# A two-layer trunk on one core: the second norm's sums from x, x·d and d², and residual, norm and split pair by pair into a feature-outermost product

## The chip, the core and the metric

The kernel runs on one core of a Trainium2 chip. The metric is the device time of one execution in microseconds (us). Of the kernel before there are three runs: 2750.5, 2752.84 and 2771.38 us, so a median of 2752.84 us. A change of under about 1% of that, some 27 us, is hardly told from no change by such runs.

## What is computed

Two layers of a transformer-like trunk act on 256 tokens (128 context tokens and 128 latent tokens, the two "groups") with 2048 features. Each layer has two sub-layers, and each of them is wrapped in two RMS norms ("sandwich"):

```python
def rmsnorm(x, g):
    y = x32 * lax.rsqrt(jnp.mean(x32 * x32, axis=-1, keepdims=True) + EPS)
    return y * g

def trunk_layer(x, mod, p, ctx, rope):
    sh1, sc1, g1, sh2, sc2, g2 = jnp.split(mod, 6, axis=-1)
    h = rmsnorm(x, p['g_pre_mix']) * (1.0 + sc1) + sh1
    mix, side = mixers(h, p, ctx, rope)        # in-projection, attention, DFT, recurrent heads
    x = x + g1 * rmsnorm(mix @ p['w_out'], p['g_post_mix'])
    h = rmsnorm(x, p['g_pre_ffn']) * (1.0 + sc2) + sh2
    x = x + g2 * rmsnorm(conv_ffn(h, p), p['g_post_ffn'])
    return x, side
```

The modulation (shift, scale, gate; one set per group) is a product of a conditioning vector with a weight of 2048 x 12288 per layer. Between two sub-layers stand, one behind the other, the norm of the sub-layer's output d, the residual addition, the norm of the new x and the modulation; the next product needs all of it.

## The kernel before

**Layout.** Features lie on partitions and tokens on columns. x is eight tiles `x[k]` of [128, 2, 256] (128x512 elements each; tile k holds features 256k to 256k+255), d is eight tiles `ds[k]` of the same form. A norm over features is thus a sum over partitions, which TensorE does with a matrix of ones.

**Products.** Each fp32 weight is split into two fp32r parts, hi (cast on ScalarE, L343) and lo (subtraction on VectorE, L344), and so is the activation h (`hx`, hi and lo). A product is three terms: hi·hi, hi·lo and lo·hi. `gemm` and `gemm_k` issue three matmuls of 256 columns (L353, L354, L355). `gemm_wide` issues two, one of 512 columns (L382) and one of 256 (L383). `gemm_k` is feature-outermost: it holds several PSUM banks open, takes the features in four pieces of 512 (two tiles of x each) from a generator, and needs a piece only when it comes to it. `gemm_wide` goes through all features for one group of 512 output columns.

**Sums.** `sumsq4` squares a tile on ScalarE (L476) and adds it with two matmuls by ones (L480), each into one of four 32-row strips of a PSUM bank: the matrix of ones has 32 columns there, where the products use 128. `strips` copies the bank (L485) and adds the strips up with one full matmul (L487). `rstd` makes the reciprocal root with two ScalarE operations (L494, L495) and three dependent VectorE operations (L496 to L498).

**Order of the work.** A tile scheduler fixes the order of each engine's instructions when the program is built, and each engine runs its list strictly in order. The modulation's weights are streamed as side work between the products (`mb` L243, `mc` L250, `mod` L255, `modx` L289). `need` takes care that those of a piece are issued by the time that piece is modulated.

**The seams.** There are three places between sub-layers: A (layer 0, mixer to FFN, about 579 to 604 us), B (layer 0 to layer 1, 1469 to 1492 us), C (layer 1, mixer to FFN, 1958 to 1983 us). Ahead of each, the last product adds up the d tiles (L1190 in A and C, L1233 and L1234 in B), and for each tile `done` squares it, sums the square and scales d by the gate (`scale_out`, L552). At the seam `post_norm` makes r1 from these sums, multiplies all d tiles (L545) and adds all into x (L546). Tiles 5 and 6 are done by GpSimd (`POOLX`), the others by VectorE. Then `pre_norm` squares and sums all eight x tiles, makes r2, and yields four pieces. For each tile a piece has four VectorE operations x·scale·r2 of 128x128 (L534), four ScalarE operations that add the shift and cast to hi (L535), and four VectorE operations for lo (L536). `pre_norm` makes the pieces of layer 0's in-projection too, where a piece also waits for its modulation weights. After A and C the first group of the FFN's up-projection is a `gemm_wide`; after B the in-projection is a `gemm_k`, and x is stored to DRAM (`spill_x`, on SyncE's queue). In the mixer x is not on chip; `fill_x` brings it back ahead of the last part of the out-projection.

## Time and profile before

The profile shows one execution of 2751.85 us by its own clock; its span in the trace is 2749.9 us.

| what | value |
|---|---|
| runs | 2750.5, 2752.84, 2771.38 us |
| the profiled execution's own time | 2751.85 us |
| its span | 2749.9 us |
| TensorE (PE) busy | 2648.2 us, 96% |
| weight loads (PEld) busy | 2138.7 us, 78% |
| VectorE (DVE) busy | 1774.9 us, 65% |
| ScalarE (ACT) busy | 1280.8 us, 47% |
| GpSimd (POOL) busy | 123.8 us, 5% |

To read it: the busy time of an engine says little about what a stage is bound by. The stages are read with windows (busy time of each engine between two moments, with TensorE's granted clock: 1.00 is 2.4 GHz, 0.50 is 1.2 GHz) and with the timeline, which lists an engine's instructions in order of time. A row of the timeline that ends with x4 stands for four like records. A plain matmul by ones has two records.

### The profile page before, as it was taken

The numbers are of one execution on the slowest core, as the hardware profiler recorded it, in microseconds if no ns is written. First come the engines' busy times: TensorE is split into PE (matmuls) and PEld (weight loads), VectorE is DVE, ScalarE is ACT, GpSimd is POOL, SyncE is SP. The second block draws the span as 40 slices with busy tenths as digits, with TensorE's granted clock in tenths as the row PEclk, the third lists the DMA queues.
The fourth block names the chain that finished last, engine by engine and source line by source line (L and its number), as shares of the span: only waits on it lengthen the run. The fifth ranks groups of instructions, "written<-read, shape, count | busy, mean of one in ns | idle before, by whom it ended". The sixth has DMA issues, their size and how long they took to land. (4 is left out here: it accounts for less than half of the span.)

```text
span 2749.9 us, 46006 instructions
## 1 busy us (share of the span) xinstructions
PE 2648.2 (96%) x18307; PEld 2138.7 (78%) x18307; DVE 1774.9 (65%) x3008; ACT 1280.8 (47%) x1985; POOL 123.8 (5%) x130
## 2 busy tenths in 40 slices
PE   7999999989999999999998999999799999999997
PEld 4577778757777777777776987878588888888886
DVE  3477858576564466555667687775777646765675
ACT  2255434245453454434544456343465545554553
POOL 1111000010000000000000020000100000000000
PEclk9999999999999999999998999998899999999998
DMA  9965636768888878888876654443355555655552
GB/s 364 382 200 171 224 119 198 252 233 279 273 266 269 283 268 271 265 275 273 267 258 204 213 186 158 153 134 116 114 183 186 193 190 190 191 190 189 189 186 82
DMA packets 316472, 593.95 MB, mean 216 GB/s; under 512 B 22758, under 2 KB 38146, under 8 KB 316256
## 3 DMA queue, kind: packets, MB, share of 16 engines
q1 hardware_dynamic: 314624, 589.54, 64.7%
q8 instruction: 144, 2.36, 0.3%
q0 software_dynamic: 1632, 1.46, 0.2%
q14 instruction: 72, 0.59, 0.1%
HBM read 583.78 MB, written 7.14 MB: 215 GB/s over the span
## 5 line engine op out<-in xcount | busy, mean ns | idle before, releaser
L344 DVE TENSOR_TENSOR lo<-raw,hi 128x1024 fp32r<-128x1024 f32 (+1 forms) x712 | 855.2, 1202 | 656.1 <-ACT hi L343 620.2
L343 ACT CAST hi<-raw 128x1024 fp32r<-128x1024 f32 (+1 forms) x712 | 734.5, 1032 | 949.5 <-PE wm L382 631.9
L382 PE MATMUL wm<-hx,hi 128*128 128x512 f32 x2816 | 994.6, 397 | 8.4 <-DVE hx L536 7.7
L383 PE MATMUL wm<-hx,lo 128*128 128x256 f32 x2816 | 787.4, 280 | 0.0
L382 PEld LDWEIGHTS wm<-hx,hi 128*128 128x128 f32 x2816 | 528.9, 188 | 174.2 <-issue 37.7
L383 PEld LDWEIGHTS wm<-hx,lo 128*128 128x128 f32 x2816 | 533.0, 189 | 3.2 <-issue 2.5
L382 PE MATMUL wm<-g,hi 128*128 128x512 f32 x1408 | 498.9, 398 | 0.0
L383 PE MATMUL wm<-g,lo 128*128 128x256 f32 x1408 | 395.6, 281 | 0.0
L382 PEld LDWEIGHTS wm<-g,hi 128*128 128x128 f32 x1408 | 264.0, 188 | 83.8 <-issue 24.7
L383 PEld LDWEIGHTS wm<-g,lo 128*128 128x128 f32 x1408 | 266.1, 189 | 7.2 <-issue 7.1
L243 PE MATMUL mb<-raw,cst 128*32 128x512 f32 x1536 | 255.9, 614 | 10.7 <-DVE mod L255 6.3
L353 PE MATMUL mm<-hx,hi 128*128 128x256 f32 x544 | 157.9, 294 | 4.2 <-ACT hx L535 4.2
L355 PE MATMUL mm<-hx,lo 128*128 128x256 f32 x544 | 155.6, 288 | 0.9 <-DVE lo L344 0.9
L354 PE MATMUL mm<-hx,hi 128*128 128x256 f32 x544 | 155.9, 288 | 0.5
L353 PE MATMUL mm<-mx,hi 128*128 128x256 f32 x512 | 155.1, 304 | 0.0
L355 PE MATMUL mm<-mx,lo 128*128 128x256 f32 x512 | 148.0, 291 | 1.3 <-DVE lo L344 1.3
L354 PE MATMUL mm<-mx,hi 128*128 128x256 f32 x512 | 148.6, 291 | 0.0
L353 PEld LDWEIGHTS mm<-hx,hi 128*128 128x128 f32 x544 | 104.4, 194 | 24.9 <-issue 14.0
L353 PEld LDWEIGHTS mm<-mx,hi 128*128 128x128 f32 x512 | 100.4, 196 | 24.9 <-issue 20.3
L355 PEld LDWEIGHTS mm<-hx,lo 128*128 128x128 f32 x544 | 105.0, 193 | 5.7 <-issue 3.5
L354 PEld LDWEIGHTS mm<-hx,hi 128*128 128x128 f32 x544 | 105.3, 194 | 4.8 <-issue 3.4
L559 ACT ACTIVATE u<-us,vec 128x256 f32<-128x256 f32 x176 | 100.4, 596 | 15.0 <-DVE us L1215 11.0
(343 smaller groups left out, 3261.4 us busy)
## 6 DMA issues: line engine op xcount, KB each, us to landing
raw<-in_w_mod SPq DMA_DIRECT2D x384, 512.0 KB, 5.2
raw<-in_ffn_w_up SPq DMA_DIRECT2D x352, 512.0 KB, 4.5
raw<-in_ffn_w_down SPq DMA_DIRECT2D x176, 512.0 KB, 4.3
raw<-in_w_in SPq DMA_DIRECT2D x80, 512.0 KB, 4.9
raw<-in_w_out SPq DMA_DIRECT2D x64, 512.0 KB, 5.1
raw<-in_w_uq SPq DMA_DIRECT2D x16, 384.0 KB, 4.5
raw<-in_w_in SPq DMA_DIRECT2D x16, 320.0 KB, 3.5
raw<-in_w_in SPq DMA_DIRECT2D x16, 256.0 KB, 3.4
```

The lines of the kernel that those rows point to most:

```text
L243: nc.tensor.matmul(b[32 * q:32 * q + 32, :], self.cst[:, 4 * kg + q, :], r[:, f, :], start=kg == 0, stop=kg == 3)
L343: nc.scalar.copy(hi[:, :, 0:w], r)
L344: nc.vector.tensor_tensor(lo[:, :, 0:w], r, hi[:, :, 0:w], op=ALU.subtract)
L353: mm(out, whi, xhi, start=start, stop=False)
L354: mm(out, whi, xlo, start=False, stop=False)
L355: mm(out, wlo, xhi, start=False, stop=stop)
L382: mm(ps[m], hi[:, kk, s], x[:, :, kk, :], start=ki == 0 and k2 == 0 and kk == 0, stop=False)
L383: mm(ps[m][:, 0, :], lo[:, kk, s], x[:, 0, kk, :], start=False, stop=ki == n - 1 and k2 == 1 and kk == 1)
L559: nc.scalar.activation(u[:, m, :], ps[:, m, :], AF.Identity, scale=w1, **kw)
```

## The change

1. Ahead of a seam, `done` now makes three sums for each tile: of d² (unscaled), of scaled d times x, and of scaled d squared. They are two squares on ScalarE (L1223, L1226) and one product on VectorE (L1225), three buffers instead of one, and six matmuls by ones in three strips (`sums3`, L474) instead of two matmuls. The last norm of layer 1 keeps `sumsq4`.
2. At a seam, `between` takes the place of `post_norm` and `pre_norm`. One copy (L480) and three matmuls (`spread3`, L484) give the three totals. r1 comes from the first. Four VectorE operations of 128x256 (L561 to L564) update the kept sum of x², `sx`, by 2·r1·(x·d) + r1²·d², and r2 comes from `sx`. No tile of x is squared or summed. d·r1 (L568) and x+d (L569) are done for the two tiles of a piece, just ahead of its modulation, all on VectorE; GpSimd has no part in it.
3. `modulate` makes h = x·r2 with one VectorE operation of 128x512 (L544), four ScalarE operations of 128x128 in place with two per-partition pointers, scale and shift (L549), one ScalarE cast to hi (L550), and one VectorE subtraction to lo (L551), 128x512 each. This form also stands at the start of layer 0, where `sx` is copied too (L528).
4. The first group of the FFN's up-projection is a `gemm_k` that takes the pieces as they come (`evu0` convolves its result from PSUM directly).

```diff
+    def sums3(self, ps, k, srcs):
+        for j in range(2):
+            for i, t in enumerate(srcs):
+                self.nc.tensor.matmul(ps[32 * i:32 * i + 32, :], self.c(C_ONE, 32), t[:, j, :], start=k == 0 and j == 0, stop=k == 7 and j == 1)
+
+    def spread3(self, ps):
+        nc = self.nc
+        sb = self.half([128, 256], nm="sb")
+        nc.scalar.copy(sb[0:96], ps[0:96])
+        out = [self.bank([128, 256]) for _ in range(3)]
+        for i, o in enumerate(out):
+            r = slice(32 * i, 32 * i + 32)
+            nc.tensor.matmul(o, self.c(C_QS, 128)[r], sb[r], start=True, stop=True)
+        return out
...
+    def modulate(self, l, which, k, rs, before=None):
...
+        for e in range(2):
+            if before:
+                before(2 * k + e)
+            hi, lo = out[e][:, 0], out[e][:, 1]
+            h = self.half([128, 2, 256], nm="h")
+            nc.vector.tensor_tensor(h, self.x[2 * k + e], self.bc(rs, 2), op=ALU.mult)
+            for j in range(2):
+                c = 4 * k + 2 * e + j
+                for g in range(2):
+                    s = slice(128 * g, 128 * g + 128)
+                    nc.scalar.activation(h[:, j, s], h[:, j, s], AF.Identity, bias=self.mod[l][:, sh0 + c, g:g + 1], scale=a[:, c, g:g + 1])
+            nc.scalar.copy(hi, h)
+            nc.vector.tensor_tensor(lo, h, hi, op=ALU.subtract)
+        return out
+
+    def between(self, ds, ss, l, which):
+        tt = self.nc.vector.tensor_tensor
+        tot, xd, dd = self.spread3(ss)
+        r1 = self.rstd(tot, D)
+        t = self.half([128, 256], nm="t")
+        tt(t, dd, r1, op=ALU.mult)
+        self.nc.vector.scalar_tensor_tensor(t, xd, 2.0, t, op0=ALU.mult, op1=ALU.add)
+        tt(t, t, r1, op=ALU.mult)
+        tt(self.sx, self.sx, t, op=ALU.add)
+        r2 = self.rstd(self.sx, D)
+
+        def add(k):
+            tt(ds[k], ds[k], self.bc(r1, 2), op=ALU.mult)
+            tt(self.x[k], self.x[k], ds[k], op=ALU.add)
         for k in range(4):
-            self.need(l, sh0 // 4 + k, sh0 // 4 + 4 + k)
-            out = [self.duo("hx") for _ in range(2)]
...
-                        nc.vector.scalar_tensor_tensor(h[:, j, s], self.x[2 * k + e][:, j, s], a[:, c, g:g + 1], rs[:, s], op0=ALU.mult, op1=ALU.mult)
-                        nc.scalar.activation(hi[:, j, s], h[:, j, s], AF.Identity, bias=sh)
-                        nc.vector.scalar_tensor_tensor(lo[:, j, s], h[:, j, s], sh, hi[:, j, s], op0=ALU.add, op1=ALU.subtract)
-            yield out
+            yield self.modulate(l, which, k, r2, add)
...
         def done(which, k):
...
-            self.sumsq4(pss[0], ds[k], 2 * k)
...
+            sq = [self.half([128, 2, 256], nm="sq") for _ in range(3)]
+            nc.scalar.activation(sq[0], ds[k], AF.Square)
             self.scale_out(l, which, k, ds[k])
+            nc.vector.tensor_tensor(sq[1], ds[k], self.x[k], op=ALU.mult)
+            nc.scalar.activation(sq[2], ds[k], AF.Square)
+            self.sums3(pss[0], k, sq)
...
-                self.finish(self.gemm_wide(i["ffn_w_up"][l], [(512 * gg, 512), (DFF + 512 * gg, 512)], h, range(4), evu))
+                cols = [(512 * gg, 512), (DFF + 512 * gg, 512)]
+                if gg == 0:
+                    self.finish(self.gemm_k(i["ffn_w_up"][l], cols, first, evu0, None))
+                else:
+                    self.finish(self.gemm_wide(i["ffn_w_up"][l], cols, h, range(4), evu))
```

**Where the sums stand.** TensorE's list ahead of seam C (`mm` are the out-projection's products, `ss` the bank of sums, `sq` the squares and products of one tile). In the kernel before, the two matmuls of a tile stand together:

```order
L355 MATMUL mm_19355<-mx_17954,lo_19360 128x256
L353 MATMUL mm_19355<-mx_17954,hi_19359 128x256
L480 MATMUL ss_19243<-sq_19332,const 32x256 x2
L354 MATMUL mm_19355<-mx_17954,hi_19359 128x256
L355 MATMUL mm_19355<-mx_17954,lo_19360 128x256
```

In the changed kernel the six of a tile stand in two places: the first, of the unscaled square, alone among the products, and the other five later, here with the first one of the next tile behind them:

```order
L340 MATMUL mm_19441<-mx_17982,hi_19445 128x256
L474 MATMUL ss_19297<-sq_19402,const 32x256
L341 MATMUL mm_19441<-mx_17982,hi_19445 128x256
...
L1133 MATMUL b_19467<-const,fs_16370 64x128 x2
L474 MATMUL ss_19297<-sq_19403,const 32x256
L474 MATMUL ss_19297<-sq_19404,const 32x256
L474 MATMUL ss_19297<-sq_19402,const 32x256
L474 MATMUL ss_19297<-sq_19403,const 32x256
L474 MATMUL ss_19297<-sq_19404,const 32x256
L474 MATMUL ss_19297<-sq_19428,const 32x256
L340 MATMUL mm_19442<-mx_17982,hi_19445 128x256
```

So a tile's sums interrupt the products more often than before, and only tiles 6 and 7, which end at the seam itself, have theirs in one piece.

**What stands at the seam.** VectorE's list at seam C, from r2 on. In the kernel before all additions are over, and the modulation's operations follow r2 directly (`nt` and `rs` are rstd's, `hx` is what the product reads):

```order
L498 SCALAR_TENSOR_TENSOR rs_19588<-nt_19589,rs_19588 128x256
L534 SCALAR_TENSOR_TENSOR h_19597<-x_19166,modx_103,rs_19588 128x128 x3
L536 SCALAR_TENSOR_TENSOR hx_19595<-h_19597,mod_101,hx_19595 128x128
L534 SCALAR_TENSOR_TENSOR h_19597<-x_19166,modx_103,rs_19588 128x128
L536 SCALAR_TENSOR_TENSOR hx_19595<-h_19597,mod_101,hx_19595 128x128 x3
```

In the changed kernel the additions of the first four tiles stand between the operations that lead to r2, and the subtraction to lo (L551) behind four multiplications by r2 and two by r1:

```order
L564 TENSOR_TENSOR sx_291<-sx_291,t_19661 128x256
L569 TENSOR_TENSOR x_19221<-x_19221,d_17025 128x512
L568 TENSOR_TENSOR d_17276<-d_17276,rs_19654 128x512
L501 SCALAR_TENSOR_TENSOR nt_19667<-rs_19666 128x256
L569 TENSOR_TENSOR x_19222<-x_19222,d_17276 128x512
L502 TENSOR_TENSOR nt_19667<-nt_19667 128x256
L568 TENSOR_TENSOR d_17276<-d_17276,rs_19654 128x512
L503 SCALAR_TENSOR_TENSOR rs_19666<-nt_19667,rs_19666 128x256
L569 TENSOR_TENSOR x_19223<-x_19223,d_17276 128x512
L544 TENSOR_TENSOR h_19677<-x_19220,rs_19666 128x512
...
L568 TENSOR_TENSOR d_17571<-d_17571,rs_19654 128x512 x2
L551 TENSOR_TENSOR hx_19673<-h_19677,hx_19673 128x2x256
```

Ahead of these rows, the four operations that make `sx` (L561 to L564) have three such additions between them.

**A piece at the start of layer 0.** ScalarE's list for layer 0's second piece, in the changed kernel: four operations on the first tile, one on the second, and only then the first tile's cast to `hx`, which TensorE waits for.

```order
L549 ACTIVATE h_671<-h_671,mod_100,modx_102 128x128 x4
L549 ACTIVATE h_679<-h_679,mod_100,modx_102 128x128
L550 CAST hx_669<-h_671 128x2x256
L549 ACTIVATE h_679<-h_679,mod_100,modx_102 128x128 x3
L330 CAST hi_765<-raw_763 128x1024
```

Before, the operation that adds the shift wrote `hx` itself, a quarter of a tile at a time. On VectorE the changed list has the multiplication of the second tile between `mod` and `modx`, on which ScalarE waits:

```order
L544 TENSOR_TENSOR h_671<-x_114,rs_284 128x512
L242 TENSOR_TENSOR mod_100<-mc_653,vec_98 128x8
L544 TENSOR_TENSOR h_679<-x_115,rs_284 128x512
L276 SCALAR_TENSOR_TENSOR modx_102<-mod_100,vec_98 128x8
L551 TENSOR_TENSOR hx_669<-h_671,hx_669 128x2x256
```

What depended on no modulation weight, the multiplication of the first tile, has moved ahead of `mod`.

## Rows read from the trace of the kernel before

**Rows 1.** The page, part 1: busy time and share of each engine.

```profile
PE 2648.2 (96%) x18307; PEld 2138.7 (78%) x18307; DVE 1774.9 (65%) x3008; ACT 1280.8 (47%) x1985; POOL 123.8 (5%) x130
```

**Rows 2.** Windows: PE, PEld, DVE, ACT, POOL busy, granted clock, DMA share, GB/s.

```profile
40.00:155.00 115.00, 110.59 (x742) 70.32 (x740) 43.73 (x84) 29.84 (x48) 7.43 (x15) 0.99 0.94 339
579.00:604.00 25.00, 14.33 (x75) 4.22 (x75) 21.18 (x38) 9.21 (x20) 6.72 (x4) 0.73 0.58 189
604.00:632.00 28.00, 26.87 (x158) 19.71 (x157) 23.84 (x67) 16.37 (x37) 0.00 (x0) 1.00 0.64 215
1469.00:1492.00 23.00, 12.44 (x69) 3.88 (x68) 19.03 (x32) 9.09 (x19) 6.63 (x4) 0.72 0.59 195
1958.00:1983.00 25.00, 10.37 (x47) 3.33 (x48) 19.56 (x34) 9.46 (x21) 6.71 (x4) 0.62 0.11 37
1983.00:2003.00 20.00, 18.38 (x90) 15.31 (x90) 17.56 (x50) 12.23 (x28) 0.00 (x0) 0.88 0.33 106
```

**Rows 3.** Timeline, PE, ahead of seam C: start, us, engine, line, operation [idle before].

```profile
1942.25 0.28 PE L355 MATMUL mm<-mx,lo 128*128 128x256 f32 x1
1942.37 0.28 PE L353 MATMUL mm<-mx,hi 128*128 128x256 f32 x1
1942.58 0.62 PE L480 MATMUL ss<-sq,const 128*32 128x256 f32 x4
...
1943.36 0.28 PE L355 MATMUL mm<-mx,lo 128*128 128x256 f32 x1
```

**Rows 4.** Timeline at seam C, all engines.

```profile
1956.11 1.42 DVE L1190 TENSOR_TENSOR d<-d,mm 128x512 f32<-128x512 f32 x2
...
1957.72 1.15 ACT L476 ACTIVATE sq<-d 128x512 f32<-128x512 f32 x2
1957.85 1.22 DVE L344 TENSOR_TENSOR lo<-raw,hi 128x1024 fp32r<-128x1024 f32 x1 [0.31 <-ACT hi L343]
...
1958.99 1.28 DVE L552 TENSOR_TENSOR d<-d,modx 128x512 f32<-128x512 f32 x2
1959.59 0.37 ACT L485 COPY sb<-ss 128x256 f32<-128x256 f32 x1 [0.73 <-PE ss L480]
...
1961.85 0.47 ACT L494 ACTIVATE rs<-b,eps 128x256 f32<-128x256 f32 x1 [1.89 <-PE b L487]
...
1963.35 0.42 DVE L498 SCALAR_TENSOR_TENSOR rs<-nt,rs 128x256 f32<-128x256 f32 x1
1963.81 2.36 DVE L545 TENSOR_TENSOR d<-d,rs 128x512 f32<-128x512 f32 x2
...
1977.65 0.70 PE L487 MATMUL b<-sb,const 128*128 128x256 f32 x2 [0.47 <-ACT sb L485]
...
1982.18 0.79 PE L382 MATMUL wm<-hx,hi 128*128 128x512 f32 x1 [3.82 <-DVE hx L536]
```

**Rows 5.** Timeline at seams A and B: the last addition into d, the first product.

```profile
578.38 0.68 DVE L1190 TENSOR_TENSOR d<-d,mm 128x512 f32<-128x512 f32 x1
...
603.53 0.51 PE L382 MATMUL wm<-hx,hi 128*128 128x512 f32 x1 [2.08 <-DVE hx L536]
...
1469.11 0.41 DVE L1234 TENSOR_TENSOR d<-d,wm 128x256 f32<-128x256 f32 x1
...
1491.37 1.01 PE L353 MATMUL mm<-hx,hi 128*128 128x256 f32 x3 [3.20 <-ACT hx L535]
```

**Rows 6.** Timeline at the start of layer 0, its second piece.

```profile
77.44 0.17 DVE L255 TENSOR_TENSOR mod<-mc,vec 128x8 f32<-128x8 f32 x1 [0.37 <-PE mc L250]
...
77.67 1.05 PE L243 MATMUL mb<-raw,cst 128*32 128x512 f32 x4 [0.29 <-DVE mod L255]
...
78.23 1.49 ACT L535 ACTIVATE hx<-h,mod 128x128 fp32r<-128x128 f32 x4 [6.62 <-DVE h L534]
...
79.60 0.50 PE L354 MATMUL mm<-hx,hi 128*128 128x256 f32 x1
```

**Rows 7.** Groups by line and form: ACT with two pointer operands, and with one.

```profile
L559 ACT ACTIVATE u<-us,vec 128x256 f32<-128x256 f32 x176 | 100.4, 596 | 15.0 <-DVE us L1215 11.0
L559 ACT ACTIVATE k<-mm,vec 128x256 f32<-128x256 f32 x8 | 3.7, 471 | 2.0 <-DVE k L563 1.3 <-PE mm L355 0.7
```

60 lines of the change are left out of this document (34 added, 26 removed).

## The prediction

> **What bounds the kernel now.** I read the page first: TensorE is busy for 96% of the span [rows 1], so nearly everything is bound by it, and other engines count only where it is idle. Then the windows [rows 2]: the idle time lies in the three seams (PE 14.33 of 25 us in A, 12.44 of 23 in B, 10.37 of 25 in C), a little behind A and C (1.1 us of 28, 1.6 of 20), and at the start, where PE has 110.59 of 115 us and the DMA share is 0.94, so there both are near their limit. The timeline then gives each seam's length, from the end of the last addition into d to the first product [rows 4, 5]: C 1982.18 − 1957.53 = 24.65 us, A 603.53 − 579.06 = 24.47, B 1491.37 − 1469.52 = 21.85. Behind C the granted clock is 0.88 in the mean [rows 2]: the first products run at the lower level, 1.2 GHz. Behind A it is 1.00, since modulation matmuls ran shortly before.
>
> So two questions decide: how much shorter the seams get, and what the longer sums cost where TensorE is busy anyway.
>
> **1. The sums ahead of the seams: +20.1.** Products follow each other every 0.12 us [rows 3]. Around one tile's sums a product that was due 0.24 us after 1942.37 starts 0.99 us after it: the block costs 0.75 us, though its four records take only 0.62. The rest is the passage into the strips and back. Two strips run at once. A second round in the same strips is not in the trace; the nearest row is the four-record block with 512 columns [rows 6], 1.05 us against 0.62 with 256, so another 256 columns in each strip cost 0.43. After the change a tile has a lone matmul (0.75: one matmul or two at once, the passage is the same) and a block of two rounds (0.75 + 0.43 = 1.18) against 0.75 before: +1.18 per tile. In A six tiles are split: +7.1. In B there are seven lone pieces and six blocks for six old blocks: 7 × 0.75 + 6 × 1.18 − 6 × 0.75 = +7.8. In C, where some lone matmuls stand behind the block of the tile before, three lone and six blocks, against four old blocks and one of two tiles, taken as 1.18: 2.3 + 7.1 − 4.2 = +5.2. Together +20.1. (Tiles 6 and 7 of each seam are in part 2.) Lowest: if a lone matmul among products cost nothing, only 18 second rounds remain, +7.7. Highest: the wait in the second rival.
>
> What speaks for the high side of this is a rule of the Trainium skill ("TensorEngine Tiling (Array Packing)", Key Properties): a change of the tiling mode, not of the tile, drains TensorE. By that rule the price goes with the number of interruptions, and the 0.13 us between 0.75 and 0.62 [rows 3] agrees that each has one; without it the sum would be nearer to +8 than to +20.
>
> The extra square and product per tile cost nothing of their own there: about 0.6 us each on engines that are not full.
>
> **2. The seams: −10.4.** I follow C from the last addition, 1957.53 [rows 4]. VectorE has one weight split, then scale, product, scale, product for tiles 6 and 7: 1.54 us until the split ends as now, then four operations of 0.60 to 0.68 (the pair takes 1.28): +4.1. With ScalarE's square beside it and two rounds of sums: +5.5. The copy starts at +5.6. From copy to root it took 2.26 us here (1959.59 to 1961.85), where a table is transposed in between, and would take 0.37 for the copy, 0.70 for the matmul and 0.1 without that: I take 1.9 at C, so +7.5, and 1.2 at A and B. Then from root to r1 1.96 as now (1961.85 to 1963.81): +9.4. Then come four operations of 256 columns at 0.46 and the three additions between them at 0.60: 3.64, so +13.1. For r2 there are three more of 0.46, five additions at 0.60 and the first multiplication 0.68: +18.1. ScalarE does four affine operations. A quarter now takes 1.49/4 with one pointer [rows 6]; a second pointer costs 596 − 471 = 125 ns [rows 7], so four take 1.49 to 2.0, I take 1.75; then the second tile's first (0.4) and the cast (0.6): hi at about +21.0. First product +21.1, against 24.65. The 1.6 us of stalls behind C go too: per piece TensorE has 96 products, 11.5 us, and VectorE about 10 (eight operations of 0.6, four weight splits of 1.22), ScalarE less. C: 21.1 − 24.65 − 1.6 = −5.1.
>
> B is one operation and the rest of a split (1.0) shorter and has the earlier root: 21.1 − 1.0 − 0.7 = +19.4, so −2.5. A is as C with the earlier root, +20.4, and loses 1.1 us of stalls; but its modulation matmuls now run ahead of the long wait, not just before the products, so it will start at 1.2 GHz as C does. Behind C 0.12 of the clock is missing over 20 us: 2.4 us, which I charge to A. A: 20.4 − 24.47 − 1.1 + 2.4 = −2.8. The three make −10.4.
>
> Bounds: if the additions slip in for free where VectorE waits for ScalarE, some 2.5 us per seam less, −18; if each dependent operation takes 0.68 rather than 0.60 and the four affine ones 2.0, 2.5 more each, −3. GpSimd's part in the additions falls away; nothing is queued behind it. At B the eight stores of x to DRAM wait in SyncE's queue for additions that now come up to 12 us after the first product; weights queued behind them are of the second piece, which starts 168 products, 20 us, after the first, and need some 5 us to land. That cover gone, it would cost up to those 5 us. The first FFN group as `gemm_k` streams the same 768 columns per block: nothing.
>
> **3. The start of layer 0: +5.** Four pieces each wait for their modulation weights. Before, the first product that needs lo came 2.16 us after `mod` started (77.44 to 79.60) [rows 6]. After: `mod` 0.17, the second tile's multiplication 0.60, `modx` 0.2, affine operations 1.75 + 0.4, cast 0.6, subtraction 0.68 and handovers 0.3 make 4.7: +2.6 at a piece with nothing else to do. In the first two, modulation matmuls that stand there cover about half (+1.5, +1.1). That is +7.8 for four. The first three lie where the DMA is near its limit [rows 2], so a late product is partly made good; I take half for them: 2.6 + 2.6 = +5. Bounds +2.6 (only the last counts) and +14 (twice the sum, with the clock falling in each gap).
>
> **Sum.** 20.1 − 10.4 + 5 = +14.7 on the profiled execution's own 2751.85 (its span is 2 us shorter) gives 2766.6; the median of the three runs is 1 us above it, so **2767 us**, 0.5% more than before.
>
> **The rivals.**
>
> *The sums are nearly free and the seams give all* (0.22). Strips would let a lone matmul slip between products. Sums +7.7, seams −18, start +2.6: −7.7, 2745 us. For it: only 0.13 of the 0.75 us is passage, and strips do run side by side. Against it: the products wait through the whole block [rows 3]. A share of 0.07 is kept for seams that shrink by 10 us each, below 2725.
>
> *TensorE waits in line for the late product* (0.15). The six matmuls of a tile need scaled d times x, which is last on VectorE, and TensorE runs its list in order. If a weight split of 1.22 us [rows 4] stands ahead of that product each time, 18 tiles wait up to 1.22: +22, so 2789 us, slower by 1.3%. It decides from a mean wait of 0.75 us per tile, which takes 2767 to 2780.4. For it: the list puts the five matmuls only some ten products (1.2 us) behind the lone one. Against it: the scheduler set the list so that the operands should be there.
>
> *The seams do not shrink* (0.13). Eight of the sixteen additions still stand between r1 and the first product, r2 still has its own root, and ScalarE now has five operations where the quarter tiles went one by one. If that eats all: 20.1 + 0 + 5, 2778 us. For it: 8 × 0.60 = 4.8 us remain in the chain. Against it: eight squares with sums, GpSimd's slow operations (one of two of VectorE's takes 2.36 − 0.60 = 1.76 beside it [rows 4]) and half of the additions are gone.
>
> **How the numbers follow.** My forecast has 0.50 and reaches from 2757 to 2779. The first rival goes from 2742 upward for most of its 0.22, the second and third up to 2789. The range 2742 to 2789 leaves out the 0.07 below 2725, some 0.06 between, and about 0.06 above: 8 in 10 inside. About 1% can be told from no change, 2725 to 2780. Faster: the 0.07. Slower: nearly all of the second rival, a third of the third, and a rest of my own, 0.20. Within 1%: 0.73.
>
> **What would show it.** Right in step 1: in the windows ahead of the seams each tile's sums hold the products up twice, about 0.75 and 1.2 us; wrong if products follow a lone sum without a gap, or if the five begin after an idle time that the product L1225 ends. Right in step 2: first products 21, 20.5 and 19.5 us after the last addition at C, A and B, a clock near 0.5 behind A, no idle time in the first FFN group. Right in step 3: PE idle 2.6 us more ahead of layer 0's last piece. The prediction is wrong as a whole if the stage ahead of a seam is not longer, or a seam not shorter.

## The result, and the profile after

The changed kernel takes 2787.12 us in the median of six runs (2784.94 to 2799.71), beside 2765.72 for the kernel before in the same rounds (2750.5 to 2771.38): a ratio of 1.0086, interval 1.0065 to 1.0107. On another chip the same pair gave 1.0127 (1.0103 to 1.015). So the change makes the kernel slower, by 21 us and 30 us between these medians; predicted were 14.7 us, too little to be told from no change. 2787 us lies near the upper end of the wide range (2742 to 2789) and outside the forecast's own 2757 to 2779.

One thing must be known to read any of these numbers: the runs of the kernel before fall into two groups, about 2751 and 2765 us, and the execution profiled ahead of the prediction is of the lower one. A second profile of the same kernel took 2764.83 us. The two differ in layer 1's feed-forward. These are windows over the same 500 us of it; the columns are those of [rows 2]. First the execution of [rows 1]:

```profile
2100.00:2600.00 500.00, 500.00 (x2886) 441.18 (x2885) 320.51 (x426) 257.79 (x334) 0.00 (x0) 1.00 0.59 190
```

The second profile of the kernel before:

```profile
2100.00:2600.00 500.00, 500.00 (x2833) 433.60 (x2832) 314.22 (x419) 252.47 (x330) 0.00 (x0) 1.00 0.62 186
```

The changed kernel:

```profile
2100.00:2600.00 500.00, 500.00 (x2832) 433.56 (x2831) 312.93 (x414) 251.03 (x327) 0.00 (x0) 1.00 0.59 187
```

TensorE is never idle and its granted clock is 1.00 in all three, but 2886 matmuls are done in the first and 2833 and 2832 in the others: a pair of one 512-column and one 256-column product takes 0.347 or 0.353 us. Over the whole of that feed-forward this is 12.6 us. It does not need the change, since both kinds occur in the kernel before. Whether the change makes the faster pace rarer was not tested: 43 of the 113 runs of the kernel before lie below 2758 us, while all sixteen profiles of other builds have the slower pace, and so has one of the changed kernel at 2786.17 us, close to the lowest of its twelve runs. All delays below are therefore taken against the second profile, whose pace is that of the changed kernel's profile (own time 2791.3 us): 2791.3 − 2764.83 = 26.5 us to explain.

Part 1 of the page, of the second profile of the kernel before and then of the changed kernel, answers to [rows 1]. At the same pace TensorE is busy 19 us longer, at the same share (31 us longer than in [rows 1], where the pace is the faster one):

```profile
PE 2660.2 (96%) x18307; PEld 2140.7 (77%) x18307; DVE 1775.8 (64%) x3008; ACT 1280.4 (46%) x1985; POOL 123.7 (4%) x130
PE 2679.2 (96%) x18665; PEld 2163.6 (78%) x18665; DVE 1756.4 (63%) x2849; ACT 1300.5 (47%) x1998; POOL 95.4 (3%) x118
```

Its windows answer to [rows 2]: the start, and for each seam the wait and what follows it.

```profile
40.00:155.00 115.00, 105.67 (x675) 70.63 (x669) 34.34 (x45) 32.81 (x52) 7.43 (x15) 0.93 0.93 332
603.00:623.00 20.00, 9.71 (x62) 3.05 (x62) 17.20 (x36) 7.09 (x17) 0.00 (x0) 0.73 0.63 224
623.00:651.00 28.00, 28.00 (x222) 27.89 (x222) 18.41 (x23) 18.42 (x33) 0.00 (x0) 0.95 0.50 152
1495.00:1513.00 18.00, 6.56 (x40) 1.48 (x40) 14.55 (x28) 5.96 (x15) 0.00 (x0) 0.63 0.72 236
1992.00:2012.00 20.00, 5.00 (x30) 1.58 (x30) 15.97 (x32) 6.95 (x16) 0.00 (x0) 0.66 0.09 30
2012.00:2032.00 20.00, 19.76 (x152) 19.66 (x153) 17.58 (x25) 19.96 (x41) 0.00 (x0) 0.92 0.35 109
```

The stalls behind A and C are gone (28.00 of 28, 19.76 of 20 us busy), and the start has become worse: 105.67 busy of 115 us in place of 110.59, at a granted clock of 0.93 in place of 0.99.

To see where time goes I took, for every VectorE and ScalarE instruction that two kernels share, the difference of its start times, and the median of it at five moments: the end of layer 0's start and mixer (500), the end of layer 0's feed-forward (1400), behind seam B (1500), the end of layer 1's mixer (1900), behind seam C (2050). Up to the end it then stays the same within 0.6 us. Around 1900 the difference is not steady (in the changed kernel some 31 us just before and 26 just after), so that column is good to about 3 us. In us, against the second profile of the kernel before:

| kernel | 500 | 1400 | 1500 | 1900 | 2050 |
|---|---|---|---|---|---|
| changed | 19.6 | 18.8 | 20.5 | 28.2 | 26.6 |
| e1, old start | 0.2 | −2.2 | 0.9 | 12.1 | 12.7 |
| e2, new start only | 17.9 | 17.9 | 17.9 | 17.9 | 17.9 |
| e3, sums together | 18.9 | 16.6 | 13.3 | 20.2 | 15.2 |
| e5, filled start | 14.7 | 12.7 | 14.5 | 35.6 | 36.1 |
| e6, e3 with old start, old seam B | 2.9 | 0.2 | −0.1 | 8.1 | 3.0 |
| e7, e3 with old start, additions late | −0.7 | −0.6 | −4.7 | 5.9 | 0.8 |
| e8, e7 with old seam B | 4.9 | 4.9 | 4.7 | 8.7 | 3.4 |
| e9, e7 with side work earlier | 3.0 | 2.7 | 1.5 | 1.7 | −3.3 |
| e10, before with side work later | −1.2 | −6.3 | −5.9 | 12.7 | 11.9 |
| e11, changed with side work earlier | 15.1 | 15.4 | 17.7 | 14.7 | 13.1 |
| e12, e9 with side work earlier still | 0.7 | 7.9 | 4.2 | 5.1 | −0.3 |
| f1, changed, second chip | 16.7 | 17.2 | 19.2 | 22.9 | 21.5 |
| f2, e11 again, f1's chip | 17.8 | 18.8 | 21.4 | 21.4 | 20.9 |
| f3, e7 again, f1's chip | 2.9 | 0.5 | −2.0 | 8.8 | 3.8 |
| f4, e9 again, f1's chip | 1.6 | 1.0 | −2.2 | −13.7 | −20.0 |

So the changed kernel loses 19.6 us at the start of layer 0, next to nothing over seams A, B and C taken with the sums ahead of them, and 7.7 us in layer 1's mixer (3.7 in its second profile, f1), which the change doesn't touch.

### The profile page after: what moved, and what is told of

It reads as the page before. It is cut to its first block, busy times and chain, and to the rows that moved or that the text cites. A ratio compares the mean times of both kernels' runs of the same rounds, so it can differ in the third digit from the quotient of the medians.

```text
span 2789.1 us, 46576 instructions
## 1 busy us (share of the span) xinstructions
PE 2679.2 (96%) x18665; PEld 2163.6 (78%) x18665; DVE 1756.4 (63%) x2849; ACT 1300.5 (47%) x1998; POOL 95.4 (3%) x118
## 4 chain that ended last, share of the span: by engine, by line
PE 87%; DVE 4%; DMA 4%; ACT 2%; issue 1%; POOL 0%; SPq 0%; ACTq 0%; DVEq 0%; POOLq 0%
PE wm L369 34%; PE wm L370 17%; PE mb L230 7%; PE mm L340 5%; PE mm L342 5%; PE mm L341 5%; DMA raw<-in_w_mod 3%; PE b L340 2%; PE b L342 2%; PE b L341 2%; PE px L1072 1%; PE ss L474 1%; PE pr L1066 1%; DMA raw<-in_w_out 1%; DVE lo L331 1%
## 5 line engine op out<-in xcount | busy, mean ns | idle before, releaser
L369 PE MATMUL wm<-hx,hi 128*128 128x512 f32 x2560 | 911.4, 400 | 0.0
L370 PE MATMUL wm<-hx,lo 128*128 128x256 f32 x2560 | 717.5, 280 | 0.0
L369 PEld LDWEIGHTS wm<-hx,hi 128*128 128x128 f32 x2560 | 480.7, 188 | 158.3 <-issue 41.1
L370 PEld LDWEIGHTS wm<-hx,lo 128*128 128x128 f32 x2560 | 483.1, 189 | 1.7 <-issue 1.7
L230 PE MATMUL mb<-raw,cst 128*32 128x512 f32 x1536 | 260.0, 620 | 18.1 <-DVE mod L242 9.3
L340 PE MATMUL mm<-hx,hi 128*128 128x256 f32 x736 | 216.3, 299 | 24.6 <-ACT hx L550 24.6
L342 PE MATMUL mm<-hx,lo 128*128 128x256 f32 x736 | 213.7, 293 | 3.1 <-DVE lo L331 3.0
L341 PE MATMUL mm<-hx,hi 128*128 128x256 f32 x736 | 215.6, 294 | 0.2 <-DVE hx L551 0.2
L340 PEld LDWEIGHTS mm<-hx,hi 128*128 128x128 f32 x736 | 146.1, 201 | 48.0 <-ACT hx L550 31.3
L341 PEld LDWEIGHTS mm<-hx,hi 128*128 128x128 f32 x736 | 146.9, 200 | 8.2 <-issue 6.6
L342 PEld LDWEIGHTS mm<-hx,lo 128*128 128x128 f32 x736 | 146.4, 200 | 5.7 <-DVE lo L331 4.7
L341 PE MATMUL mm<-mx,hi 128*128 128x256 f32 x512 | 146.5, 287 | 0.0
L340 PEld LDWEIGHTS mm<-mx,hi 128*128 128x128 f32 x512 | 97.7, 191 | 27.2 <-issue 23.2
L341 PEld LDWEIGHTS mm<-mx,hi 128*128 128x128 f32 x512 | 98.1, 192 | 6.4 <-issue 6.1
```

The costliest lines, as they stand in the source:

```text
L230: nc.tensor.matmul(b[32 * q:32 * q + 32, :], self.cst[:, 4 * kg + q, :], r[:, f, :], start=kg == 0, stop=kg == 3)
L340: mm(out, whi, xhi, start=start, stop=False)
L341: mm(out, whi, xlo, start=False, stop=False)
L342: mm(out, wlo, xhi, start=False, stop=stop)
L369: mm(ps[m], hi[:, kk, s], x[:, :, kk, :], start=ki == 0 and k2 == 0 and kk == 0, stop=False)
L370: mm(ps[m][:, 0, :], lo[:, kk, s], x[:, 0, kk, :], start=False, stop=ki == n - 1 and k2 == 1 and kk == 1)
```

## The experiments

In the words on record, theory 1 (1a) is that the start costs more than the sum gave it, by its waits and by the clock behind them; theory 2, that seam B's new order delays layer 1's mixer; theory 3, that the additions in the chain lengthen the seams; theory 4, that side work slipped into the mixer.

**The kernel before, a second profile.** No edit.

> The kernel before once more, for a second trace of it. Its six runs lie in two groups, 2750 to 2753 and 2764 to 2771. In the profiled one a pair of matmuls in layer 1's FFN took 0.347 us, in the changed kernel 0.353. If that pitch is a mode of an execution and not of the change, an execution of the kernel before at 2764 or more shows 0.353 too, and one at 2753 or less 0.347. If it comes from the change, every execution of the kernel before shows 0.347.

2764.83 us. It showed the two paces of the feed-forward above.

**The start alone, and the change without it.** e2 is the kernel before with the new modulation in layer 0's in-projection only; e1 is the changed kernel with the old modulation there. One form of the edit, e2's:

```diff
             hi, lo = out[e][:, 0], out[e][:, 1]
             h = self.half([128, 2, 256], nm="h")
+            if l == 0 and which == 0:
+                nc.vector.tensor_tensor(h, self.x[2 * k + e], self.bc(rs, 2), op=ALU.mult)
...
+                nc.scalar.copy(hi, h)
+                nc.vector.tensor_tensor(lo, h, hi, op=ALU.subtract)
+                continue
```

> The changed kernel with one part undone: the four pieces at the start of layer 0 are modulated in the form of the kernel before (quarter tiles, shift and cast in one ScalarE operation). Theory 1, from the two traces: that start lost 18 us (each piece's wait is 2 to 3 us longer, and TensorE's granted clock falls to 1.2 GHz behind each), so this runs about 18 us below the changed kernel, near 2769, and the trace agrees with that of before within 2 us up to 500 us. Theory 0, my forecast: the start costs 5 us, so 5 us below, near 2782.

> The kernel before with one part of the change alone: the four pieces at the start of layer 0 are modulated in the new form (multiplication of a whole tile, four affine ScalarE operations, cast, subtraction). Theory 1: 18 us above the kernel before. Theory 0, my forecast: 5 us above. A third way: the granted clock fell by chance in the one profile of the changed kernel; then some 8 us, the longer waits alone.

e2: 2782.84 us, ratio 1.0073 (1.0044 to 1.0101), and a delay of 17.9 us that is complete at 400 us. e1: 2780.18 us, 1.0063 (1.004 to 1.0086), and a delay of 0.2 at 500. By e2's median and by both traces the start is thus worth 18 to 19 us, where +5 stood in the sum. e1's median does not show it: it lies 7 us below the changed kernel's, on another chip, where 18 were expected. Its profile lost 11.2 us in layer 1's mixer, and its runs reach from 2766.66 to 2785.84 us. Over the whole start, the second profile of the kernel before:

```profile
0.00:400.00 400.00, 373.86 (x3208) 279.35 (x3209) 244.30 (x532) 165.30 (x314) 49.98 (x61) 1.00 0.71 245
60.00:180.00 120.00, 115.45 (x823) 80.12 (x820) 59.08 (x121) 41.31 (x72) 9.36 (x16) 1.00 0.87 309
```

And e2, to the same landmark 18 us later:

```profile
0.00:418.00 418.00, 386.26 (x3208) 289.98 (x3209) 237.18 (x484) 171.78 (x322) 45.69 (x61) 0.96 0.69 234
60.00:180.00 120.00, 109.65 (x721) 73.94 (x718) 39.78 (x56) 35.84 (x57) 7.43 (x15) 0.93 0.80 281
```

The same 3208 matmuls: idle time grows by 5.6 us (26.1 to 31.7), and busy time by 12.4, with the clock at its lower level, 1.2 GHz, for 3 to 7 us at each wait. The DMA share falls from 0.87 to 0.80 between 60 and 180 us, and little of the lost time comes back: from the `mod` of one piece to that of the next e2 takes 2.0 us longer between the first two, but 4.7 and 4.9 us longer behind the second and third.

The waits for the cast, as the view of waits totals them (engine, line and what it waits for: us, times, longest). The kernel before, 30 to 182 us:

```profile
PE mm L353 <- ACT hx L535: 1.0, 4, 0.3
```

The changed kernel, 30 to 200 us:

```profile
PE mm L340 <- ACT hx L550: 8.8, 4, 2.2
```

And one of the four in its timeline, the second piece, which answers to [rows 6]:

```profile
80.16 0.16 DVE L242 TENSOR_TENSOR mod<-mc,vec 128x8 f32<-128x8 f32 x1
...
80.83 0.16 DVE L276 SCALAR_TENSOR_TENSOR modx<-mod,vec 128x8 f32<-128x8 f32 x1
81.03 2.03 ACT L549 ACTIVATE h<-h,mod,modx 128x128 f32<-128x128 f32 x5 [4.50 <-DVE modx L276]
...
82.97 0.60 ACT L550 CAST hx<-h 128x512 fp32r<-128x512 f32 x1
...
83.62 0.79 PE L340 MATMUL mm<-hx,hi 128*128 128x256 f32 x2 [2.18 <-ACT hx L550]
...
84.34 0.58 PE L341 MATMUL mm<-hx,hi 128*128 128x256 f32 x1
...
84.94 0.41 PE L340 MATMUL mm<-hx,hi 128*128 128x256 f32 x1
85.15 0.41 PE L341 MATMUL mm<-hx,hi 128*128 128x256 f32 x1
```

The first product that needs lo (L341) starts 84.34 − 80.16 = 4.2 us after `mod`, where 4.7 was worked out and 2.16 stood before: the wait itself was sized well, a little high. The four waits grew from 1.0 to 8.8 us, by the 7.8 that the prediction had before it halved three of them. Behind it products follow each other every 0.21 us instead of 0.12.

**The waits filled.** e5 is the changed kernel with ten idle matmuls by zero ahead of each of the last three pieces, so that TensorE does not stand still there. They add nothing to the result.

```diff
+            if kg and not self.filled[kg]:
+                self.filled[kg] = 1
+                for n in range(FILL):
+                    m = self.nc.tensor.matmul(banks[0][0][:, 0, 0:64], self.c(C_ONE, 128), self.zero, start=False, stop=False)
...
```

> The changed kernel with ten idle matmuls (a zero operand, 64 columns, added into an open bank, so that nothing changes) ahead of each of the last three pieces of layer 0's start, held back until ScalarE begins on that piece. They fill TensorE's wait and change no other engine's work. Theory 1a: of the 18 us that the start lost, about half is the granted clock, which falls to 1.2 GHz behind each longer wait; with the waits filled it stays at 2.4 GHz, and the trace is 6 to 10 us ahead of the changed kernel's at 400 us. Theory 1b: the waits alone make the 18 us; then no difference, or 1 us more for the fillers themselves.

Windows of e5, as those of e2 above:

```profile
0.00:414.70 414.70, 387.13 (x3273) 289.34 (x3274) 237.82 (x486) 171.47 (x322) 42.72 (x61) 0.99 0.69 237
60.00:180.00 120.00, 115.81 (x803) 77.55 (x802) 42.23 (x60) 37.49 (x60) 7.43 (x15) 1.00 0.81 284
```

The clock is at 2.4 GHz (1.00) between 60 and 180 us, and the start is 4.9 us shorter than in the changed kernel (14.7 against 19.6), a little under the 6 to 10 expected. The waits' own time stays, now filled, and the idle matmuls cost something themselves: in these pieces the first product comes 4.79, 3.67 and 4.79 us after `mod`, beside 3.46 in the changed kernel, 2.9 us in all. So the lower clock behind three of the four waits is worth 4.9 us, seen by taking it away, or some 8 by the estimate that adds those 2.9. Of e2's 17.9 us the trace gives 5.6 to idle time and 12.4 to longer busy time. (The total of 2801.44 us is no measure of the start: this execution lost 21 us in layer 1's mixer, where it was at the lower clock for longer.)

**The sums of a tile kept together.** e3 is the changed kernel, with the first matmul of a tile's sums made to wait for the tile's last operand.

```diff
...
-            nc.vector.tensor_tensor(sq[1], ds[k], self.x[k], op=ALU.mult)
-            nc.scalar.activation(sq[2], ds[k], AF.Square)
-            self.sums3(pss[0], k, sq)
+            p = nc.vector.tensor_tensor(sq[1], ds[k], self.x[k], op=ALU.mult)
+            q = nc.scalar.activation(sq[2], ds[k], AF.Square)
+            self.sums3(pss[0], k, sq, (p, q))
```

> The changed kernel with the six matmuls of a tile's sums kept together: the first waits for the last of its three inputs to be ready, so none stands alone among the products. Theory of the passage (each interruption of the products by a strip matmul costs about 0.75 us, however few columns it has): 18 lone ones fewer, 18 x 0.75 = 13.5 us below the changed kernel. Rival, by columns alone: the same six matmuls stream the same columns, so no difference beyond 2 us.

2785.21 us, 1.0088 (1.0053 to 1.0123): in the total the 13.5 us expected do not show. In the trace a part of them does. The stage from the first to the last addition into d was 31.7, 68.1 and 24.1 us ahead of A, B and C. It is 36.4, 74.0 and 29.3 in the changed kernel (+4.7, +5.9, +5.2: 15.8), and 35.9, 68.9, 27.5 in e3 (+4.1, +0.8, +3.4: 8.3). In TensorE's timeline ahead of C, the changed kernel, a lone sum and a block:

```profile
1972.88 0.28 PE L340 MATMUL mm<-mx,hi 128*128 128x256 f32 x1
1973.09 0.62 PE L474 MATMUL ss<-sq,const 128*32 128x256 f32 x2
1973.64 0.38 PE L341 MATMUL mm<-mx,hi 128*128 128x256 f32 x1
1973.86 0.28 PE L342 MATMUL mm<-mx,lo 128*128 128x256 f32 x1
...
1985.29 0.28 PE L342 MATMUL mm<-mx,lo 128*128 128x256 f32 x1
1985.50 1.06 PE L474 MATMUL ss<-sq,const 128*32 128x256 f32 x12
1986.49 0.39 PE L340 MATMUL mm<-mx,hi 128*128 128x256 f32 x1
1986.71 0.28 PE L341 MATMUL mm<-mx,hi 128*128 128x256 f32 x1
```

And e3, all six of a tile:

```profile
1968.53 0.28 PE L340 MATMUL mm<-mx,hi 128*128 128x256 f32 x1
1968.73 1.06 PE L474 MATMUL ss<-sq,const 128*32 128x256 f32 x12
1969.73 0.39 PE L341 MATMUL mm<-mx,hi 128*128 128x256 f32 x1
1969.95 0.28 PE L342 MATMUL mm<-mx,lo 128*128 128x256 f32 x1
```

Against a product every 0.12 us, the first product behind the lone sum is 0.64 us late (1973.64 − 1972.88 − 0.12) and the second, as the prediction measured it, 0.74 (1973.86 − 1972.88 − 0.24). Behind a block the second product is 1.18 us late, in e3 (1969.95 − 1968.53 − 0.24) as in the changed kernel, where this block has five matmuls of one tile and the first of the next. So taking a lone sum into the block of its tile saves its whole price. There are 15 interruptions less in e3, five ahead of A, seven ahead of B and three ahead of C, and they gave 0.6, 5.1 and 1.8 us, 7.5 in all. At 0.74 each this comes out at B (5.2) and nearly at C (2.2), but not at A (3.7), where TensorE is idle for 1.5 us in e3 and for 0.1 in the changed kernel. The rule that stood against the change, that a new tiling mode drains TensorE (the Trainium skill, "TensorEngine Tiling (Array Packing)", Key Properties), agrees in kind. No idle time stands in front of a block that the product L1225 ends: the second rival did not happen.

**The seam before layer 1, old.** e3 had shown that seams and sums come out near zero, but not where the 7 to 11 us in layer 1's mixer come from (table, 1500 to 1900). Theory 2 was that seam B's new order delays them. e6 has the old start, the sums together and the old seam B.

```diff
...
-            for t in self.pre_norm(l, 0) if l == 0 else self.between(*self.pending, l, 0):
+            for t in self.pre_norm(l, 0):
...
```

> The changed kernel with the old modulation at layer 0's start, with each tile's sums together, and with seam B (layer 0 to layer 1) as in the kernel before, sums, additions and modulation. Theory 2: the mixer of layer 1, which ran 8 us longer in the trace of the changed kernel (between 1570 and 1930 us), did so because the changed seam B made the scheduler set that mixer's lists in another order; with the old seam B it takes what it took before, within 1 us. Rival: it is longer because of TensorE's clock there or of the changed seam A; then 6 us or more stay. In all by theory 2: seams A and C win 5 us each and pay 3 us each for sums, so 4 us below the kernel before; by the rival 3 us above it.

2762.92 us, 1.0017 (0.9996 to 1.0038). Layer 1's mixer still loses 8.2 us: theory 2 fell.

**The additions held back.** e7 is e6 with the new seam B, and with the additions of pieces 2 to 4 placed behind the second multiplication by r2 (L544) of the piece before them, which `hs` keeps. e8 is e7 with the old seam B.

```diff
...
-            tt(ds[k], ds[k], self.bc(r1, 2), op=ALU.mult)
+            w = tt(ds[k], ds[k], self.bc(r1, 2), op=ALU.mult)
+            if k >= 2:
+                self.tc.add_manual_dep(w.ins, self.hs[k // 2 * 2 - 1].ins.name, mybir.DependencyInfo(mybir.DependencyClass.NoSync, mybir.DependencyReason.DATA), reason="just in time")
```

> The changed kernel with the old modulation at layer 0's start, with each tile's sums together, and with the additions of the second to fourth pieces held back until the multiplications by r2 of the piece before are issued, so that four instead of eight additions stand between r1 and the first product at each seam. Theory 3: these additions are on the chain that sets the end of a seam, 4 x 0.6 = 2.4 us each: first products 18, 17.3 and 15.9 us after the last addition into d at C, A and B, instead of 20.35, 19.7 and 18.3. Rival: they fill time in which VectorE waits for ScalarE's root, and the seams stay within 0.5 us.

> The same as the kernel with the late additions, with seam B as in the kernel before. If theories 1, 2 and 3 and the price of the passage all hold, seams A and C win 7 us each and pay 3 us each for sums: 8 us below the kernel before, 0.3%, which a median of ten runs can just about show. If the mixer of layer 1 stays longer, no better than the kernel before.

e7: 2765.56 us, 1.0012 (0.9992 to 1.0032); e8: 2767.3, 1.0021 (1.0 to 1.0042). At seam C of e7:

```profile
1967.15 0.68 DVE L1256 TENSOR_TENSOR d<-d,mm 128x512 f32<-128x512 f32 x1
...
1985.34 1.01 PE L340 MATMUL mm<-hx,hi 128*128 128x256 f32 x3 [10.62 <-ACT hx L572]
```

17.5 us from the end of the last addition to the first product, as expected, beside 18.4 in e3; at A 17.4 beside 19.3, at B 16.1 beside 18.1. So the additions that stood in the chain cost 1 to 2 us per seam by these two profiles; in a second profile of e7's program (f3) the three are 17.5, 16.6 and 17.5 at C, A and B, so a figure for one seam is good to about 1 us. In the total of about 2765 us e6, e7 and e8 cannot be told apart, and e8 did not win the 8 us that were one of its two expectations: its mixer still loses 4.0.

**The side work.** The weight matmuls of the modulation (`mb`) are issued by an allowance that grows with the products, and by `need`. The first group of the feed-forward is now a `gemm_k`. Its pieces call `need` later, when the allowance has already issued a part of what they ask for, so fewer steps are issued ahead of layer 1: between the first product behind A and the last addition ahead of B there are 704 records of `mb` where there were 712, and in seam B itself, where TensorE stands idle anyway, 8 where there were 16. TensorE's `mb` group in layer 1's mixer (line, operation, count, busy us and mean ns, idle before), from seam B's first product to about 1930 us in the kernel before:

```profile
L243 PE MATMUL mb<-raw,cst 128*32 128x512 f32 x176 | 28.1, 604 | 1.8 <-DVE mod L255 1.8
```

and in the same stretch of the changed kernel:

```profile
L230 PE MATMUL mb<-raw,cst 128*32 128x512 f32 x192 | 38.1, 642 | 2.6 <-DVE mod L242 2.6
```

Sixteen records more, 10 us more busy time, some of it at the lower clock (mean 642 ns in place of 604). Theory 4 says that this is the mixer's loss. e9 is e7 with three steps of allowance added behind the first feed-forward group; e10 is the kernel before with three taken away there; e11 is the complete changed kernel with three added; e12 is e9 with six.

```diff
                     self.finish(self.gemm_k(i["ffn_w_up"][l], cols, first, evu0, None))
+                    if l == 0:
+                        self.credit += 3
```

> This is the kernel with the old start, the sums of a tile kept together, the additions of pieces 2 to 4 held back and all seams new, with one number changed: behind the first feed-forward group of layer 0 the allowance of side work is raised by three steps, so that the modulation matmuls are issued where the kernel before issues them (680 of them ahead of layer 1's first projection and 716 at the end, where the last build had fewer). Theory 4 (the 8 us that layer 1's mixer lost are modulation work pushed out of layer 0's feed-forward and into the mixer): the delay against the kernel before grows by at most 1 us between 1550 and 1900 us, where it grew by 6 to 10 in the last builds; layer 0's feed-forward gets back at most 4 us of matmuls; the whole is 5 to 7 us below the build with the held-back additions in the same feed-forward pace. Rival (the loss in the mixer comes from the new order of instructions in general): the growth stays 6 or more and the total is the same within 1 us.

> The kernel before with one number changed: behind the first feed-forward group of layer 0 the allowance of side work is lowered by three steps, so that the modulation matmuls are issued as late as in the changed kernel (672 ahead of layer 1's first projection). Sums, seams and the start are the old ones. Theory 4: the delay against the kernel before grows by about 8 us between 1550 and 1900 us, after about 4 us were won in layer 0's feed-forward, so the total is about 4 us longer. Rival (the lateness of side work is only a move of it): what the feed-forward wins the mixer loses, and the total is 0 within 1 us.

> The changed kernel, complete (new start, sums tile by tile as they come, all seams new), with one number added: behind the first feed-forward group of layer 0 the allowance of side work is raised by three steps, as in the build with the modulation work put back. Theory 4 (8 of the changed kernel's microseconds are modulation matmuls and their DMA waits that slipped into layer 1's mixer): the delay against the kernel before, 18.8 us at 1400 us, grows by at most 2 between 1550 and 1900 us where it grew by 8 in the changed kernel, and the whole is 6 to 9 us shorter than the changed kernel. Rival (with the new start the allowance is used elsewhere, or the wait only moves): the whole is shorter by less than 3 us.

> The build with the modulation work put back, but with six steps of allowance added in place of three: 24 modulation matmuls more in layer 0's feed-forward, ahead of where the kernel before has them. Theory 4 in its narrow form (only late side work costs, since it then waits for its own transfers at the end of layer 1's mixer, and at the old place that wait is gone): the feed-forward pays up to 6 us for 24 matmuls of 0.25 us, the mixer wins the same back and no wait, so the whole is the same within 2 us as with three steps. Rival (each step of side work that leaves layer 1's mixer is worth more there than it costs in the feed-forward): layer 1's mixer gets shorter by 8 or more and the whole by 4 or more.

| kernel | median us | ratio to before | growth 1500 to 1900 |
|---|---|---|---|
| e9 | 2748.25 | 0.9965 (0.9942 to 0.9987) | 0.2 |
| e10 | 2771.99 | 1.0028 (1.0006 to 1.005) | 18.6 |
| e11 | 2785.54 | 1.009 (1.0059 to 1.0122) | −3.0 |
| e12 | 2763.58 | 0.9996 (0.9974 to 1.0019) | 0.9 |

The growth in the mixer is there in each build that issues the modulation late and in none that issues it early, the kernel before included, where three steps taken away make it (e10). Theory 4 holds for the stage. More than the old place is not better: e12 pays 7.2 us in layer 0's feed-forward and behind it wins 8.2 where e9 wins 6.0; neither of its two expectations held. The sizes were not those expected: e10's feed-forward won 5 us, its mixer lost 18.6 in place of 8, again with more time at the lower clock, and its median is 8 us longer where 4 were expected. What the total gains was less clear: 17 us from e7 to e9, far more than expected, but 1.6 from the changed kernel to e11, and on different chips. So the four went on one chip together.

> The changed kernel again, as the partner of the next run on the same chip. Theory 4: about 26 us over the kernel before in the same feed-forward pace, and 6 to 13 us over the next run. Rival (the earlier work is undone elsewhere when the start is the new one): the next run is within 3 us.

> The changed kernel with three steps of allowance for side work added behind layer 0's first feed-forward group, on the same chip as the changed kernel. Theory 4: 6 to 13 us below it. Rival: within 3 us of it.

> The build with the old start, the sums of a tile together, the additions of pieces 2 to 4 held back and the new seams, as the partner of the next run on the same chip. Theory 4: equal to the kernel before within 3 us, and 5 to 8 us over the next run. Rival (the 17 us between the two medians were the chips): within 3 us of the next run.

> The same build with three steps of allowance for side work added behind layer 0's first feed-forward group, on the same chip. Theory 4: 5 to 8 us below the partner, and 3 to 6 below the kernel before. Rival: within 3 us of the partner.

f1 2788.92 us (1.0127, 1.0103 to 1.015), f2 2785.19 (1.0107, 1.0082 to 1.0131): 3.7 us, between what theory and rival said, and the intervals overlap, so unresolved. In their profiles, too, the delay at 2050 differs by 0.6 us only (21.5 and 20.9): that the mixer's loss is a part of the complete kernel's time is shown for its stage and not for its total. f3 2766.1 (1.0022, 1.0 to 1.0043), f4 2747.52 (0.9977, 0.9954 to 1.0): 18.6 us, as from e7 to e9 and far above the 5 to 8 expected. In f2's trace the group is back at its old size:

```profile
L230 PE MATMUL mb<-raw,cst 128*32 128x512 f32 x176 | 28.1, 604 | 1.7 <-DVE mod L242 1.7
```

Why the same three steps bring 18 us in the builds with the old start, where the mixer's growth is 6 to 11 us, f4's profile shows in part. e9 and f4 are the same program; e9's profile took 2761.61 us and f4's 2744.29. At the mixer's end, first the second profile of the kernel before, then e9:

```profile
1879.00:1907.00 28.00, 28.00 (x205) 25.27 (x203) 8.89 (x14) 4.97 (x7) 3.34 (x6) 0.51 0.16 49
1862.00:1881.00 19.00, 18.22 (x161) 14.87 (x160) 16.25 (x36) 7.61 (x17) 0.00 (x0) 1.00 0.62 200
1881.00:1909.00 28.00, 28.00 (x200) 25.19 (x197) 8.89 (x14) 4.81 (x7) 3.34 (x6) 0.51 0.15 49
```

and f4:

```profile
1860.00:1879.00 19.00, 18.23 (x167) 15.71 (x164) 15.58 (x33) 8.01 (x17) 0.00 (x0) 1.00 0.67 209
1879.00:1894.00 15.00, 15.00 (x189) 13.40 (x188) 8.21 (x14) 4.40 (x6) 3.33 (x6) 1.00 0.22 65
```

The same work takes 28 us at 1.2 GHz, in the kernel before too, or 15 at 2.4. Seven of the twelve runs of e9, and seven of f4's, are below 2750 us; of e7 and f3 together one of 24 is. The runs below 2750 have a granted clock of 0.984 to 0.987 over the whole execution, the other runs of e9 and f4 0.975 to 0.983, and the kernel before 0.976 to 0.982 in all but one of its 107 runs in the experiments' rounds. So it is likely that the runs below 2750 are those without this stretch, though a profile shows it once only, and much of what this build wins is the clock. What makes the clock fall there in one execution and not in the other stays open: TensorE is busy 18.2 of the 19 us ahead of it in both.

## Why the prediction was wrong

**What bounds the kernel** was read rightly: TensorE, and the other engines where it stands still.

**Step 1, the sums (+20.1): right in kind, a quarter too high.** The stages grew by 15.8. The prices were right: measured as the prediction did, to the second product behind, the block of two rounds costs 1.18 us and the lone sum 0.74, where 1.18 and 0.75 were taken. So C came out as worked out, 5.2. A cost 4.7 in place of 7.1: lone sums there stand directly beside a block of side work, and two of them lengthen that interruption by 0.41 us only (1.50 in place of 1.09). B cost 5.9 in place of 7.8: TensorE was idle for 1.5 us in that stage of the second profile of the kernel before, and not at all in the changed kernel's.

**Step 2, the seams (−10.4): right in direction, half as much again came.** The first products came 19.7, 18.3 and 20.4 us after the last addition at A, B and C; 20.4, 19.4 and 21.1 were worked out. At C:

```profile
1991.20 0.69 DVE L1232 TENSOR_TENSOR d<-d,mm 128x512 f32<-128x512 f32 x1 [0.75 <-PE mm L342]
...
1998.59 0.37 ACT L480 COPY sb<-ss 96x256 f32<-96x256 f32 x1 [1.99 <-PE ss L474]
...
2008.93 2.49 DVE L544 TENSOR_TENSOR h<-x,rs 128x512 f32<-128x512 f32 x4
2009.64 2.03 ACT L549 ACTIVATE h<-h,mod,modx 128x128 f32<-128x128 f32 x5 [3.71 <-DVE h L544]
...
2011.58 0.60 ACT L550 CAST hx<-h 128x512 fp32r<-128x512 f32 x1
2012.24 1.01 PE L340 MATMUL mm<-hx,hi 128*128 128x256 f32 x3 [12.52 <-ACT hx L550]
```

Counted from the addition's end, the copy starts at 6.7 us (5.6 was worked out), the first multiplication by r2 at 17.0 (17.4), and the product at 20.4 (21.1). The stalls behind A and C went, as foreseen. Behind A the products start at the lower clock, as foreseen (0.95 over 28 us), but the 2.4 us charged for it were hardly a loss: the second profile of the kernel before has 0.96 there, where [rows 2] have 1.00.

```profile
604.00:632.00 28.00, 26.79 (x150) 19.57 (x150) 22.77 (x63) 15.27 (x35) 0.00 (x0) 0.96 0.60 195
```

The operation with two pointers (L549) has a median of 480 ns, the old one with one (L535) 388, both 128x128: 92 ns more, where 125 was read from rows whose inputs also differ. From the table and the stages the three seams and their stalls make −16.0: A −1.3 − 4.7 = −6.0, B 2.7 − 5.9 = −3.2, C −1.6 − 5.2 = −6.8 (A's −1.3 and B's 2.7 from the delays just around them, 18.3 at 700 us and 17.8 at 1350). Sums and seams together come to −0.2, where +9.7 was predicted.

**Step 3, the start (+5): this step failed.** It cost 18 to 19. The waits were sized right (7.8 us more, as worked out for the four together). What failed is the clock: its fall at each wait, 12.4 us of longer busy time in e2's trace and so more than the waits themselves, was put only into the upper bound of +14, though [rows 2] show it behind C, and the same prediction charged it to A. Halving the first three waits because the DMA is near its limit there found little support: time was made good between the first two pieces and not behind them, and the DMA share fell from 0.87 to 0.80. That the idle time grew by 5.6 us in all, close to the +5, came about in part because other waits of TensorE became shorter, those of `mb` for its weights from 3.2 us to 1.2 in e2 (30 to 200 us). By the highest bound as it stood the sum would have been 2776.

**What no step had: the side work.** Layer 1's mixer lost 7.7 us (28.2 − 20.5). The first feed-forward group was costed at nothing because it streams the same columns. But as a `gemm_k` it also decides when the modulation's pieces are asked for, and the steps that it no longer draws into layer 0's feed-forward and seam B came up in the mixer. The instruction order of both kernels would have shown it: 16 records of `mb` stand behind seam B's first product that stood ahead of it. The 7.7 are one profile's; f1's has 3.7.

Put together: 19.6 − 0.5 (layer 0's feed-forward) + 15.8 − 16.0 + 7.7 = 26.6, the table's last column. On the prediction's base of 2751.85 us this would be 2778; the other 13 us up to the changed profile's 2791.3 are the slower pace, of which the prediction had one sign, the run of 2771.38 us. That 2787 still falls into the range is luck in part: steps 1 and 2 were 4.3 and 5.6 us too high, which took off some of the 14 us that step 3 was short and of the mixer's 7.7.

**The rivals.** None of the three happened. The sums were not free, TensorE did not wait for the late product, and the seams did shrink. The time came out near the second rival's 2789 for reasons that are not its own. The first measurement, 0.86% slower, lies within the 1% that had 0.73, the one on the other chip, 1.27%, beyond it, where 0.20 stood; one case does not say whether these chances were of the right size.

**A version a little better than both.** e9, which is f4: the old start, a tile's sums together, the additions just in time, the new seams, and the side work at its old place. 0.9965 (0.9942 to 0.9987) and 0.9977 (0.9954 to 1.0) of the kernel before, some 6 to 10 us; the second interval reaches 1, and in the profile of e9, with the slow stretch that the kernel before has too, the gain is 3.3 us.

## What to carry to other kernels

Where a change puts waits of 2 us into a stretch in which TensorE is otherwise busy, price the products behind each wait at the lower clock as well, from a stretch of the same trace where that is seen; here this was 12.4 us beside 5.6 of added idle time. When a loop is exchanged for one that "streams the same columns", look at what else its progress drives: side work issued by an allowance moves with it, and a difference of the two instruction orders, counted per stage, shows where to. And compare a profile with another profile of the same kernel before explaining it: 13 of the 39 us between the first two profiles here are also found between two profiles of the kernel before.

## What the runs showed of the hardware

- In the kernel before, a pair of a 512-column and a 256-column product takes 0.347 or 0.353 us, for the whole of layer 1's feed-forward, at a granted clock of 1.00 and without idle time. It differs between two executions of that kernel and is worth 12.6 us.
- In e2, each of four idle times of 2.2 us ahead of layer 0's pieces came with 3 to 7 us at 1.2 GHz; with idle matmuls in three of them (e5) the clock stayed at 2.4 GHz there.
- The same program (e9 and f4), with TensorE busy 18.2 of 19 us beforehand, went through the end of layer 1's mixer at 1.2 GHz in one execution (28 us) and at 2.4 in another (15 us).
- A lone matmul by a 32-column matrix of ones made the second product behind it 0.74 us late, six of them in three strips 1.18.
